# Gates and half of q as seven products of halves per pair of column tiles, with V and the gates kept in DRAM

## The chip, the core and the metric

The kernel runs on one core of one Trainium2 chip. The core has five engines with queues of their own: TensorE (PE) multiplies, VectorE (DVE), ScalarE (ACT) and GpSimd (POOL) work on tiles, and SyncE (SP) issues most of the transfers between DRAM and the core's memory (SBUF). Matmul results go to PSUM, eight banks of 128x512 float32 numbers. Each engine takes its instructions in the order in which the program has them and waits on semaphores for the others. The metric is the device time of one execution in microseconds (us), the median of several runs.

## What is computed

One layer on 1024 tokens of 1024 features, with 16 learned meta tokens ahead of them, in float32. The normed rows u go through one wide projection, and three branches are gated and merged; a mixture of experts follows.

```python
p = u @ w_in
a, bv, bg, q, k, v, fg, gates = jnp.split(p, ...)
ya = pool_mixer(a, ...) @ w_out_a
yb = conv_module(bv, bg, ...) @ w_out_b        # 31 taps, layer norm, swish
logf = jax.nn.log_sigmoid((fg + b_forget).astype(jnp.float32))
yc = forgetting_attention(heads(q), heads(k), heads(v), logf) @ w_out_c
g = jax.nn.sigmoid(gates.reshape(B_, L, N_BRANCH, D))
merged = g[:, :, 0] * ya + g[:, :, 1] * yb + g[:, :, 2] * yc
h = h + merged @ w_o
h = h + hier_moe(rms_norm(h))                   # 16 experts, two of a group's four for a token
```

The gates are 3 x 1024 columns of the projection, 24 column tiles of 128; q, k and v have four each, a, bv and bg two each.

## The kernel before

Float32 accuracy comes from two parts of each operand. A helper, split, makes the high part on ACT (a cast, L167) and the low part on DVE (a subtraction, L168); mm3 (L173) then multiplies high by high, low by high and high by low. A column tile of the projection for 512 tokens is 8 blocks of features times 3 kinds, 24 matmuls of 128x128 by 128x512. The normed u lies transposed in four tiles (two high, two low), each with four blocks of 1040 tokens.

The projection is a list of jobs, run by run_jobs in order, with the weights of a job loaded and split some jobs ahead. The order is bg, bv and a, then four times K and Q of a pair of heads, the 16 gate tiles of branches A and B, V with the forget gate, and the 8 gate tiles of branch C, the last of them among the first attention scores. Each K and Q goes to DRAM (dq, dk) as high and low part. Vector work of the pooling branch and of the convolution is queued in a list, pending: the pooling, 60 taps (L446), the layer norm (L455 to L498, with matmuls against ones at L460 for sums over channels). Its pieces are taken off the list ("pumped") a few at a time behind each job; before the gates the list is emptied.

A gate tile's sigmoid (L548) meets its branch at once: mm_bk gets a product with w_out_a or w_out_b (6 matmuls a half tile), DVE multiplies (L554, L557), POOL adds (L558). The merged rows (mg4) and the gates of C stay in SBUF, as V does. Attention works in units of a head's half, in blocks of 128 tokens: scores (L754, L755), exp, transposes (L803), weighing of V (L812, L814); heads are loaded by SP (L716 to L723) one ahead. Behind it the third branch (L860 to L872) and the output projection (L1095) follow, then routing and experts. SBUF is handed out in 12 equal slots; a freed slot goes to the next taker, whose first write waits for the last use. The order of instructions on an engine is settled when the program is built, so it can differ a little from the order in the source.

Of the kernel before, what the change touches and what calls it, by code (L numbers as in the profile page):

```python
# [7 lines left out]
F32 = mybir.dt.float32  # L8
# [33 lines left out]
def view(a, off, shape, dt=None):  # L42
    """A piece of a [P, n] tile, from column `off`, in `shape`"""
    n = 1
    for s in shape:
        n *= s
    a = a[:, off:off + n]
    if dt is not None:
        a = a.bitcast(dt)
    if len(shape) == 2:  # L50
        a = a.rearrange("p (a b) -> p a b", b=shape[1])
    elif len(shape) == 3:
        a = a.rearrange("p (a b c) -> p a b c", b=shape[1], c=shape[2])
# [15 lines left out]
class Slot:  # L69
    """A tile whose columns are handed out from the left"""  # L70
# [35 lines left out]
class Banks:  # L106
    """A ring over PSUM banks, `span` neighbours at a time."""
# [14 lines left out]
def body(tc, A, out):  # L122
# [3 lines left out]
    with es:  # L126
# [48 lines left out]
        def rms_stats(src, rows_, junk, st):  # L175
            """st[:, 2] <- 1/sqrt(mean(src^2) + eps)"""
# [46 lines left out]
        class UTile:  # L223
            """a tile of tokens on its way into u"""
# [66 lines left out]
        # background vector work, put between the matmul groups  # L291
# [76 lines left out]
        def run_jobs(js):  # L368
            """each job's weights are got ready `look` jobs ahead of it"""
# [18 lines left out]
        def start_b(_):  # L388
# [8 lines left out]
            queue_conv()  # L397

# [4 lines left out]
        def queue_pool():  # L403
# [31 lines left out]
            pending.append(lambda: s_at.free())  # L435

        def queue_conv():
# [13 lines left out]
            def both(x, ct):  # L451
                """the sum of the two halves of the channels, in two parts; they lie where the result will"""
# [23 lines left out]
            def ln_var():  # L476
# [8 lines left out]
                # 1 / sqrt, with a Newton step after the table's root  # L485
# [18 lines left out]
            pending.extend([ln_sum, ln_mean, ln_var, lambda: ln_out(0), lambda: ln_out(1), ln_free])  # L504

        for hp in range(4):
            def kq(w, hp=hp, which=0):
# [20 lines left out]
        def MG(dt):
            return st["mg4"][dt // 4][:, dt % 4, :]

        job(lambda: None, start_g)

        def gate(w, dt, c):
            g = proj(w, *REAL_CHUNKS[c])
            return g

        def out_unit(wname, nk, dt):
            wv = A[wname][0].rearrange("(k p) c -> p k c", p=P)
            return load_unit(wv[:, :, dt * P:(dt + 1) * P], nk, P, st["wr"])

        def branch(b, dt, w, wy, y, nk):
            yh, yl = y[:, 0], y[:, 1]
            hy, ly = wy
            for c in range(2):
                cs = slice(c * 512, c * 512 + 512)
                g = proj(w, *REAL_CHUNKS[c])
                sg = st["sig"].next([512])
                ac.activation(sg, g, AF.Sigmoid)  # L548
                o = mm_bk.next()
                mm3(o, [hy[:, k, :] for k in range(nk)], [ly[:, k, :] for k in range(nk)],  # L550
                    [yh[:, k, cs] for k in range(nk)], [yl[:, k, cs] for k in range(nk)])
                m = MG(dt)[:, cs]
                if b == 0:
                    ve.tensor_mul(m, sg, o)  # L554
                else:
                    t = st["prd"].next([512])
                    ve.tensor_mul(t, sg, o)  # L557
                    gp.tensor_add(m, m, t)  # L558

        for b, wn, key in ((0, "w_out_a", "yaT"), (1, "w_out_b", "ybT")):  # L560
            for dt in range(KT):
                def comp(w, b=b, dt=dt, key=key, wn=wn):
                    branch(b, dt, w, out_unit(wn, 2, dt), st[key], 2)
                job(lambda b=b, dt=dt: win_unit(COL_G + b * D + dt * P), comp)

# [1 line left out]
        def start_v(_):  # L567
            st["s_ya"].free(), st["s_yb"].free(), st["s_mi"].free()
            # V by heads, high and low part side by side
            st["s_vo"] = [sl.take(F32R), sl.take(F32R)]  # L570
            st["vo"] = [x.new([2, 2 * S]) for x in st["s_vo"]]
# [6 lines left out]
        def v_put(o, m, j, h0, nh, d0, d1):  # L578
            """heads h0.. of V, columns d0 to d1 of each, from o: both parts into their place"""
            if j == 8:  # L580
                hi, lo = (st["v8"][:m, h0:h0 + nh, t, d0:d1] for t in range(2))
            else:
                v = st["vo"][h0 // 4].rearrange("p q (j h t d) -> p q j h t d", j=8, h=2, t=2)
                v = v[:m, :, j] if nh == 4 else v[:m, h0 // 2 % 2, j]
                if nh == 1:
                    v = v[:, h0 % 2:h0 % 2 + 1]
                hi, lo = (v[:, :, :, t, :] if nh == 4 else v[:, :, t, d0:d1] for t in range(2))
            if nh == 4 and j < 8:
                o = o.rearrange("p (q h d) -> p q h d", h=2, d=HD)
            else:  # L590
                o = o.rearrange("p (h d) -> p h d", d=d1 - d0)
            split(o, hi, lo)
# [1056 lines left out]
```

## Time and profile before

| | |
|---|---|
| median of 3 runs | 1184.94 us (1184.16 to 1185.47) |
| span of the profiled execution | 1188.1 us |
| PE busy in it | 1084.6 us, 91%, 5585 matmuls |
| DVE, ACT, POOL busy | 713.7, 462.0, 316.4 us |
| granted TensorE clock, 240 to 400 us | 1.00 |

The profile is of one execution, the span is its time from first to last instruction, and it lies a little above the median of the timed runs. A page of it gives busy times and the costliest groups; the trace can also be asked for a timeline of one engine, for windows of time with the busy time of each engine, and for groups by line and shape. [...] In a timeline row an entry in brackets is idle time before the row and what ended it.

### The profile page before, as it was taken

Reading aid. Unit: us, or ns where it says so; the run is one execution under the profiler, and the core shown is the slowest. Engines: PE = TensorE matmul, PEld = TensorE weight load, DVE = VectorE, ACT = ScalarE, POOL = GpSimd, SP = SyncE. Lnnn points to the kernel's source line nnn. Section 1 sums busy time; section 2 is a strip of 40 time slices with the busy share of each in tenths; the row PEclk is TensorE's granted clock in tenths of the full one; section 3 lists DMA queues with packets and bytes.
Section 4 is the critical chain, followed back from the end, with each engine's and each line's share of the span. In section 5 each row is a group of like instructions: output and inputs, shape, how many; then the busy total and the mean of one; then the engine's idle time right before and its main releaser. Section 6 shows DMA issues by size and latency. Waiting matters only on the chain. (4 is left out here: it accounts for less than half of the span.)

```text
span 1188.1 us, 15991 instructions
## 1 busy us (share of the span) xinstructions
PE 1084.6 (91%) x5585; PEld 903.8 (76%) x5585; DVE 713.7 (60%) x1274; ACT 462.0 (39%) x845; POOL 316.4 (27%) x399
## 2 busy tenths in 40 slices
PE   5999999999999999999999999899956988988872
PEld 5999897888888898887888878677745766766651
DVE  5799965712112223112888867677786955758864
ACT  5412224311122123223888852322324634536541
POOL 4001221000111200001333226200143844635654
PEclk9999999999999999999999999999967989989986
DMA  7412443211111110105855242633576896786963
GB/s 224 119 54 89 130 147 98 67 45 45 45 46 41 46 44 4 37 1 126 207 136 134 65 133 98 213 143 142 178 261 216 269 311 169 186 275 190 298 219 141
DMA packets 92547, 160.13 MB, mean 135 GB/s; under 512 B 10625, under 2 KB 59858, under 8 KB 92420
## 3 DMA queue, kind: packets, MB, share of 16 engines
q1 hardware_dynamic: 82356, 130.08, 35.5%
q0 software_dynamic: 9632, 26.94, 8.5%
q10 hardware_dynamic: 432, 1.57, 0.4%
q8 instruction: 61, 1.00, 0.3%
q14 instruction: 66, 0.54, 0.1%
HBM read 127.97 MB, written 37.33 MB: 139 GB/s over the span
## 5 line engine op out<-in xcount | busy, mean ns | idle before, releaser
L173 PE MATMUL ps<-slot,slot 128*128 128x512 f32 (+3 forms) x2016 | 423.9, 369 | 0.9 <-ACT slot L247 0.9
L173 PEld LDWEIGHTS ps<-slot,slot 128*128 128x128 f32 x2016 | 358.0, 189 | 59.2 <-ACT slot L247 1.4
L168 DVE TENSOR_TENSOR slot<-slot,slot 128x1024 fp32r<-128x1024 f32 (+2 forms) x146 | 189.2, 1322 | 141.8 <-PE ps L173 124.8
L167 ACT CAST slot<-slot 128x1024 fp32r<-128x1024 f32 (+2 forms) x163 | 151.9, 974 | 197.5 <-PE ps L173 115.2
L173 PE MATMUL ps<-slot,sm 128*128 128x512 f32 x468 | 133.8, 429 | 29.6 <-DVE sm L1344 27.9
L1328 PE MATMUL ps<-slot,slot 128*128 128x512 f32 x552 | 140.3, 411 | 14.2 <-PEq L1610 7.0
L1328 PEld LDWEIGHTS ps<-slot,slot 128*128 128x128 f32 x552 | 107.4, 198 | 45.2 <-issue 13.2
L173 PEld LDWEIGHTS ps<-slot,sm 128*128 128x128 f32 x468 | 93.0, 205 | 54.9 <-DVE sm L1344 32.4
L168 DVE TENSOR_TENSOR slot<-ps,slot 128x512 fp32r<-128x512 f32 (+3 forms) x174 | 85.9, 515 | 36.3 <-ACT slot L167 35.3
L1095 PE MATMUL ps<-slot,slot 128*128 128x512 f32 x384 | 98.5, 401 | 1.5 <-ACT slot L167 1.5
L167 ACT CAST slot<-ps 128x512 fp32r<-128x512 f32 (+3 forms) x174 | 75.2, 449 | 50.0 <-PE ps L607 23.7
L168 POOL TENSOR_TENSOR slot<-slot,slot 128x1024 fp32r<-128x1024 f32 x32 | 83.6, 2632 | 4.3 <-ACT slot L167 4.0
L1095 PEld LDWEIGHTS ps<-slot,slot 128*128 128x128 f32 x384 | 68.7, 188 | 14.5 <-ACT slot L167 1.9
L446 DVE SCALAR_TENSOR_TENSOR slot<-slot,c,slot 128x1024 f32<-128x1024 f32 x60 | 74.9, 1278 | 0.6
L558 POOL TENSOR_TENSOR slot<-slot,slot 128x512 f32<-128x512 f32 x16 | 21.4, 1335 | 197.1 <-DVE slot L557 197.1
L760 DVE CUSTOM_DVE_ANT_0 slot<-ps,slot 128x656 f32<-128x656 f32 (+7 forms) x64 | 49.4, 772 | 33.2 <-PE ps L755 19.7
L803 PE MATMUL ps<-const,slot 128*128 128x128 f32 x352 | 59.1, 276 | 0.9 <-ACT slot L692 0.4
L548 ACT ACTIVATE slot<-ps 128x512 f32<-128x512 f32 x32 | 19.2, 600 | 94.6 <-PE ps L173 92.2
L762 ACT ACTIVATE slot<-slot,sm 128x656 f32<-128x656 f32 (+7 forms) x64 | 50.8, 794 | 10.5 <-DVE sm L760 10.4
L607 PE MATMUL ps<-slot,slot 128*128 128x260 f32 (+1 forms) x432 | 51.7, 282 | 0.0
L607 PEld LDWEIGHTS ps<-slot,slot 128*128 128x128 f32 (+1 forms) x432 | 50.5, 178 | 1.2
L803 PEld LDWEIGHTS ps<-const,slot 128*128 128x128 f32 x352 | 41.9, 140 | 8.4 <-issue 1.4
(275 smaller groups left out, 1333.6 us busy)
## 6 DMA issues: line engine op xcount, KB each, us to landing
slot<-in_exp_w_dram SPq DMA_DIRECT2D x96, 512.0 KB
slot<-in_w_in_dram SPq DMA_DIRECT2D x38, 512.0 KB
slot<-dk SPq DMA_DIRECT2D x32, 260.0 KB
slot<-in_x_dram SPq DMA_DIRECT2D x16, 512.0 KB
slot<-dF SPq DMA_DIRECT2D x8, 520.0 KB
dq<-slot POOLq DMA_DIRECT2D x16, 256.0 KB, 2.3
slot<-dq SPq DMA_DIRECT2D x16, 256.0 KB
slot<-in_w_o_dram SPq DMA_DIRECT2D x8, 512.0 KB
```

The source lines that it names most:

```text
L167: ac.copy(hi, raw)
L168: (lo_eng or ve).tensor_sub(lo, raw, f32(hi))
L173: pe.matmul(o, a, b, start=i == 0, stop=i == len(ops) - 1)
L446: ve.scalar_tensor_tensor(acc[:, ct, :], src, wk, acc[:, ct, :], ALU.mult, ALU.add)
L548: ac.activation(sg, g, AF.Sigmoid)
L558: gp.tensor_add(m, m, t)
L607: pe.matmul(o, u, w, start=i == 0, stop=i == len(ops) - 1)
L760: ve.tensor_tensor_reduce(out=s2, in0=o, in1=n2, scale=-1.0, scalar=3.0e38, op0=ALU.add, op1=ALU.min, accum_out=mn)
L762: return lambda: ac.activation(s[:, 0:w], s[:, 0:w], AF.Exp, bias=mn, scale=-1.0, accum_out=sm[:, 8 + i:9 + i])
L803: pe.transpose(tp[:, t * P:(t + 1) * P], p_of(g, i0 + t)[:, b * P:(b + 1) * P], ident)
L1095: pe.matmul(o[:, c, :], a, b, start=n == 0, stop=n == 23)
L1328: pe.matmul(o, x[:, k, :], wk, start=q == 0 and i == 0, stop=q == 1 and i == len(ops) - 1)
```

## The change

Two column tiles next to each other (256 columns of weights) times two halves of the tokens and two halves of the features form a product of 2x2 blocks. It was made with eight products of blocks and is now made with seven, with sums of blocks on both sides (the scheme of Strassen and Winograd). Four sums of weights (s1 to s4) are made per pair by POOL; the sums of quarters of u are the same for all pairs and are made once on DVE (queue_sums and the head of seven): tq[3], tq[2] and tq[4], each in high and low part, and one that overwrites a quarter of u. Scratch for them, x and y, lies in one slot, s_wx, which later serves as the ring for the weights' sums. PSUM collects products that share terms; a partial result is copied out (kept) and added (joined) where it enters two results. Thirteen pairs are made so: column tiles 2 and 3 of q, and the 24 gate tiles.

The order is now bg, bv and a, four K tiles, V with the forget gate, two q tiles, the thirteen pairs. V (dv) and the gates' sigmoids (dg) are written to DRAM and read back; so are the results of the pooling and the convolution (dy, by spill). Attention follows the last pair. The products of A and B with w_out_a and w_out_b stand behind attention now, ahead of those of C.

```diff
+        dv = dr.tile([S, NH * 2 * HD], F32, name="dv")
+        dg = dr.tile([3, KT, P, S], F32, name="dg")
+        dy = [dr.tile([P, 4 * S], F32, name=f"dy{b}") for b in range(2)]
...
+        def spill(b, key):
+            x = st["s_" + key]
+            sy.dma_start(dy[b], f32(x.ap[:, 0:4 * S]))
+            x.free()
...
             pending.extend([ln_sum, ln_mean, ln_var, lambda: ln_out(0), lambda: ln_out(1), ln_free,
+                            lambda: spill(1, "yb")])
...
+        def queue_sums():
+            def begin():
+                st["s_t"] = [sl.take(F32R) for _ in range(3)]
+                st["s_wx"] = sl.take()
...
+                st["x"], st["y"] = (view(st["s_wx"].ap, o, [4, 512]) for o in (2048, 0))
...
+            def parts(n, of):
+                return [lambda: ac.copy(tq[n][0], st[of]),
+                        lambda: ve.tensor_sub(tq[n][1], st[of], f32(tq[n][0]))]
+            pending.extend(diff("x", 1, 1, 0, 1, "y") + parts(3, "x") + diff("x", 0, 1, 0, 0, "y") +
+                           less("y", 1, 1, "x") + parts(2, "y") + less("y", 1, 0, "y") + parts(4, "y"))
...
+        for hp in range(4):
+            qk_job(COL_K, hp, 0, 13)
...
+        job(lambda: [win_unit(COL_V + half * 260, 260, k0, k0 + 4) for half in range(2) for k0 in (0, 4)], v_all, 1)
...
+        job(lambda: None, forget)
+        qk_job(COL_Q, 0, 1, 4, 1)
+        qk_job(COL_Q, 1, 1, 4)
+        PAIRS = [("q", 2)] + [(b, dt) for b in range(3) for dt in range(0, KT, 2)]
+        def seven():
+            pump(1000)
+            ac.copy(uq(0, 0, 1), st["x"])
+            ve.tensor_sub(uq(1, 0, 1), st["x"], f32(uq(0, 0, 1)))
+            right = {1: (uq(0, 0, 0), uq(1, 0, 0)), 2: (uq(0, 1, 0), uq(1, 1, 0)), 3: (uq(0, 1, 1), uq(1, 1, 1)),
+                     4: tq[4], 5: (uq(0, 0, 1), uq(1, 0, 1)), 6: tq[2], 7: tq[3]}
+            st_raw = Ring([s_raw.ap[:, n * 2048:n * 2048 + 2048] for n in range(2)])
+            st_sum = Ring([st["s_wx"].ap[:, n * 2048:n * 2048 + 2048] for n in range(2)])
...
+                gp.tensor_sub(s3, a[0, 0], a[1, 0])
+                gp.tensor_add(s1, a[1, 0], a[1, 1])
+                gp.tensor_sub(s2, s1, a[0, 0])
+                gp.tensor_sub(s4, a[0, 1], s2)
...
+            def bank(n, m):
+                return ps[:, (5 if (len(PAIRS) - 1 - n) % 2 == 0 else 0) + {2: 1, 7: 2, 4: 2}.get(m, 0), :]
+            def product(n, m):
...
+                ops = [(x, y, k) for x, y in ((hi, rh), (lo, rh), (hi, rl)) for k in range(4)]
...
+            def kept(n, key, m):
+                tmp[n, key] = t_r.next([512])
+                ac.copy(f32(tmp[n, key]), bank(n, m))
...
+                ac.activation(t, x, AF.Sigmoid)
+                sy.dma_start(dg[b, i + d, :, cs], t)
...
+            for n in range(len(PAIRS)):
+                order += [(n, 7), (n, 6), (n, 2), (n, 5)]
+                if n + 1 < len(PAIRS):
+                    order.append((n + 1, 1))
+                order += [(n, 3), (n, 4)]
...
+                if n == len(PAIRS) - 1:
+                    if m == 6:
...
+                        attention_start()
+                    if m == 5:
+                        s_u[0].free(), s_u[2].free()
+                        load_v()
+                        first_scores()
...
+        def load_branches():
+            for q in range(2):
+                sy.dma_start(st["mg4"][q], dg[0, q * 4:q * 4 + 4].rearrange("k p s -> p k s"))
+            for b in range(2):
+                sy.dma_start(f32(s_br[b].ap[:, 0:4 * S]), dy[b])
...
+        def unit_out(n):
...
+                if b == 0:
+                    ve.tensor_mul(m, m, o)
+                else:
+                    t = gates[n][:, cs]
+                    ve.tensor_mul(t, t, o)
+                    gp.tensor_add(m, m, t)
...
+        def load_gate(n):
+            if KT <= n < len(units):
+                gates[n] = gate_r.next([S])
+                sy.dma_start(gates[n], dg[units[n][0], units[n][1]])
...
+        for n in range(4, 2 * KT):
+            unit_out(n)
+            if n >= KT:
+                load_gate(n + 4)
```

How the order of instructions changes is shown at three places; a row gives the line in the kernel, the operation, output and inputs, the size, and the semaphores it waits for. First DVE around the end of the layer norm, in the kernel before (slot_1417 is the result of the convolution in two parts, slot_746 its work, slot_1463 the merged rows):

```order
L495 TENSOR_TENSOR slot_746<-slot_746,slot_93 128x1024 [waits DVE_49]
L495 TENSOR_TENSOR slot_746<-slot_746,slot_93 128x1024
L496 TENSOR_SCALAR slot_746<-slot_746,c_2_71 128x1024 [waits DVE_49] x2
L168 TENSOR_TENSOR slot_88<-slot_86,slot_87 128x1024 [waits DMAHW1_49,PE_49,Activation_49]
L498 TENSOR_TENSOR slot_746<-slot_746 128x1024 [waits Activation_49] x2
L168 TENSOR_TENSOR sm_24_1466<-slot_1465,sm_24_1466 128x256 [waits DMAHW7_49,PE_49]
L168 TENSOR_TENSOR slot_1417<-slot_746,slot_1417 128x1024 [waits Activation_49] x2
L554 TENSOR_TENSOR slot_1463<-slot_1465,ps 128x512 [waits DVE_49]
L554 TENSOR_TENSOR slot_1463<-slot_1465,ps 128x512 x2
L554 TENSOR_TENSOR slot_1463<-slot_1465,ps 128x512 [waits Activation_49]
L554 TENSOR_TENSOR slot_1463<-slot_1465,ps 128x512 [waits PE_49,Activation_49]
```

Behind the last split into slot_1417 come the products with the first gates. In the changed kernel (slot_1720 is the convolution's result, slot_1907 the scratch for the sums, slot_93 to slot_96 are u, slot_1905 is tq[3]) the same place reads:

```order
L509 TENSOR_TENSOR slot_750<-slot_750 128x1024 [waits Activation_49] x2
L1140 CAST c_54_5602<-c_54_5602 128x8 [waits Pool_49]
L172 TENSOR_TENSOR slot_1720<-slot_750,slot_1720 128x1024 [waits Activation_49]
L689 TENSOR_TENSOR slot_749<-ps,slot_749 128x512 [waits PE_49,Activation_49]
L172 TENSOR_TENSOR slot_1720<-slot_750,slot_1720 128x1024 [waits Activation_49]
L700 SCALAR_TENSOR_TENSOR slot_749<-slot_749 128x512 [waits Activation_49]
L535 TENSOR_TENSOR slot_1907<-slot_94,slot_93 128x2048 [waits DMAHW5_49,DVE_49]
L536 TENSOR_TENSOR slot_1907<-slot_96,slot_95 128x2048
L537 TENSOR_TENSOR slot_1907<-slot_1907 128x2048 [waits DVE_49]
L536 TENSOR_TENSOR slot_1907<-slot_95 128x2048 [waits DVE_49]
L546 TENSOR_TENSOR slot_1905<-slot_1907,slot_1905 128x2048 [waits Activation_49]
L535 TENSOR_TENSOR slot_1907<-slot_93 128x2048 [waits DVE_49]
```

The sums of u follow the last split. The wait on DMAHW5 in the first of them is for the store of slot_1720 to DRAM on SP (L445), whose place in SBUF slot_1907 takes.

Second, PE at the layer norm's matmuls (L460; slot_89 to slot_92 are u, slot_87 and slot_88 parts of weights, slot_747 and sm_24 those of the pooling branch and its output weights), before:

```order
L173 MATMUL ps<-slot_89,slot_88 128x512 x4
L173 MATMUL ps<-slot_90,slot_88 128x512 x4
L173 MATMUL ps<-slot_89,slot_87 128x512 [waits DVE_49]
L173 MATMUL ps<-slot_89,slot_87 128x512 x3
L173 MATMUL ps<-slot_90,slot_87 128x512 x4
L460 MATMUL ps<-slot_1417,ones_80 128x512 [waits Activation_49]
L460 MATMUL ps<-slot_1417,ones_80 128x512
L173 MATMUL ps<-slot_747,sm_24_1466 128x512 [waits Activation_49]
L173 MATMUL ps<-slot_747,sm_24_1466 128x512 x2
L460 MATMUL ps<-slot_1417,ones_80 128x512 [waits DVE_49]
L460 MATMUL ps<-slot_1417,ones_80 128x512
```

They stand among the first gate tiles. In the changed kernel those matmuls (L471) stand right behind V, and further on, behind the q tiles, the first of the seven products (L680, slot_91 and slot_92 the parts of the weights) read:

```order
L680 MATMUL ps<-slot_95,slot_91 128x512 x4
L680 MATMUL ps<-slot_94,slot_92 128x512 [waits DVE_49]
L680 MATMUL ps<-slot_94,slot_92 128x512 x3
L680 MATMUL ps<-slot_96,slot_91 128x512 x4
L680 MATMUL ps<-slot_93,slot_91 128x512
L680 MATMUL ps<-slot_93,slot_92 128x512 x4
L680 MATMUL ps<-slot_95,slot_91 128x512 x4
L680 MATMUL ps<-slot_1905,slot_91 128x512 [waits Activation_49]
L680 MATMUL ps<-slot_1905,slot_91 128x512 x3
L680 MATMUL ps<-slot_1905,slot_92 128x512 [waits DVE_49]
L680 MATMUL ps<-slot_1905,slot_92 128x512 x3
L680 MATMUL ps<-slot_1905,slot_91 128x512 x4
```

The first product with a sum of u (slot_1905) is the fourth, and waits for ACT.

Third, SP around the loads of head 1, before (L191 loads weights, L716 to L718 a head's q and k, L723 its forget terms):

```order
L191 DMA slot_86<-in_w_in_dram 128x8x128 [waits DMAHW2_49,DVE_49]
L191 DMA slot_86<-in_w_in_dram 128x8x128 [waits DMAHW3_49,DVE_49]
L716 DMA slot_3495<-dq 64x1024 [waits DMAHW4_49,DMAHW3_49,DMAHW5_49,DMAHW2_49,DVE_49]
L717 DMA slot_3495<-dk 64x1040
L718 DMA slot_3495<-dk 64x1040 [waits DMAHW6_49]
L716 DMA slot_3495<-dq 64x1024 [waits DMAHW7_49]
L717 DMA slot_3495<-dk 64x1040 [waits DMAHW0_49]
L718 DMA slot_3495<-dk 64x1040 [waits DMAHW1_49]
L723 DMA slot_3562<-dF 128x656 [waits DMASW0_49,PE_49]
L723 DMA slot_3562<-dF 128x1040
L723 DMA slot_3562<-dF 128x656 [waits DMAHW4_49,DMAHW2_49,DVE_49]
L716 DMA slot_3633<-dq 64x1024 [waits DMAHW5_49,PE_49]
```

and in the changed kernel (L707 writes gates, L750 reads V, L773 to L775 a head's q and k):

```order
L707 DMA dg<-slot_749 128x512 [waits DMAHW7_49,Activation_49]
L707 DMA dg<-slot_749 128x512 [waits DMAHW0_49,Activation_49]
L750 DMA slot_3437<-dv 128x8x256 [waits DMASW7_49,DMASW6_49,DMAHW1_49,DMASW3_49,PE_49]
L750 DMA slot_3437<-dv 128x8x256 [waits DMAHW2_49]
L750 DMA slot_3438<-dv 128x8x256 [waits DMAHW3_49,PE_49]
L750 DMA slot_3438<-dv 128x8x256 [waits DMAHW4_49]
L707 DMA dg<-slot_749 128x512 [waits DMAHW5_49,Activation_49]
L707 DMA dg<-slot_749 128x512 [waits DMAHW6_49,Activation_49]
L773 DMA slot_3499<-dq 64x1024 [waits DMAHW7_49,DVE_49,PE_49]
L774 DMA slot_3499<-dk 64x1040 [waits DMAHW0_49]
L775 DMA slot_3499<-dk 64x1040 [waits DMAHW1_49]
L773 DMA slot_3499<-dq 64x1024 [waits DMAHW2_49]
```

The four reads of V have come in ahead of head 1, whose loads are those into slot_3499, and the last gates are written between.

## Rows read from the trace of the kernel before

**Rows 1.** The page's head, and part 1: busy us, share and instructions by engine.
```profile
span 1188.1 us, 15991 instructions
...
PE 1084.6 (91%) x5585; PEld 903.8 (76%) x5585; DVE 713.7 (60%) x1274; ACT 462.0 (39%) x845; POOL 316.4 (27%) x399
```

**Rows 2.** Windows by stage: us, busy of PE, PEld, DVE, ACT, POOL; clock, DMA, GB/s.
```profile
189.00:414.00 225.00, 224.83 (x973) 181.95 (x972) 73.40 (x87) 54.02 (x77) 21.40 (x18) 1.00 0.18 50
414.00:470.00 56.00, 55.86 (x449) 53.48 (x448) 15.79 (x60) 16.20 (x52) 2.12 (x3) 1.00 0.11 29
470.00:558.00 88.00, 86.83 (x377) 69.65 (x378) 11.65 (x29) 19.16 (x29) 5.14 (x34) 1.00 0.17 42
```

**Rows 3.** Timeline of PE: start, us, line, tiles, matmuls.
```profile
120.90 68.06 PE L173 MATMUL ps<-slot,slot 128*128 128x400 f32 x360
188.80 1.10 PE L460 MATMUL ps<-slot,ones 128*128 128x512 f32 x4
...
232.81 5.73 PE L173 MATMUL ps<-slot,slot 128*128 128x512 f32 x24
238.38 1.55 PE L173 MATMUL ps<-slot,sm 128*128 128x512 f32 x6
```

**Rows 4.** Windows of DVE's early and later work, columns as in rows 2.
```profile
60.00:100.00 40.00, 40.00 (x254) 39.99 (x253) 39.66 (x36) 7.05 (x12) 0.00 (x0) 1.00 0.14 40
...
240.00:400.00 160.00, 160.00 (x692) 129.75 (x691) 34.40 (x47) 30.91 (x46) 17.49 (x13) 1.00 0.16 44
```

**Rows 5.** Timeline of DVE in the layer norm: start, us, line, operation.
```profile
190.80 2.47 DVE L473 SCALAR_TENSOR_TENSOR slot<-ps,slot 128x512 f32<-128x512 f32 x4
...
211.94 0.69 DVE L490 TENSOR_SCALAR slot<-slot 128x1024 f32<-128x1024 f32 x1
...
213.93 2.36 DVE L495 TENSOR_TENSOR slot<-slot,slot 128x1024 f32<-128x1024 f32 x2
...
222.72 2.35 DVE L168 TENSOR_TENSOR slot<-slot,slot 128x1024 fp32r<-128x1024 f32 x2
```

**Rows 6.** The page's costliest groups: busy, mean ns of one, idle before.
```profile
L558 POOL TENSOR_TENSOR slot<-slot,slot 128x512 f32<-128x512 f32 x16 | 21.4, 1335 | 197.1 <-DVE slot L557 197.1
...
L607 PE MATMUL ps<-slot,slot 128*128 128x260 f32 (+1 forms) x432 | 51.7, 282 | 0.0
```

**Rows 7.** The page's DMA issues: count, KB each, us to landing.
```profile
dq<-slot POOLq DMA_DIRECT2D x16, 256.0 KB, 2.3
```

**Rows 8.** Windows of transfers, attention and clock, columns as in rows 2.
```profile
600.00:700.00 100.00, 96.68 (x643) 84.30 (x642) 83.64 (x194) 85.30 (x199) 29.29 (x84) 1.00 0.50 125
...
870.00:880.00 10.00, 1.93 (x9) 1.40 (x8) 8.94 (x38) 2.84 (x5) 3.26 (x3) 0.50 0.84 297
880.00:890.00 10.00, 6.92 (x23) 5.62 (x24) 9.19 (x13) 3.93 (x5) 8.12 (x6) 0.52 0.87 302
...
565.00:575.00 10.00, 8.53 (x57) 7.07 (x56) 7.77 (x18) 7.68 (x20) 3.22 (x10) 1.00 1.04 241
```

**Rows 9.** Groups by line and shape, ACT and DVE: busy, mean ns of one.
```profile
L167 ACT CAST slot<-slot 128x1024 fp32r<-128x1024 f32 x131 | 131.3, 1047 | 144.4 <-PE ps L173 97.2 <-PEq L1610 12.7 <-issue 10.0
...
L167 ACT CAST slot<-slot 128x512 fp32r<-128x512 f32 x28 | 16.9, 618 | 35.1 <-DVE slot L870 15.0 <-PE ps L1095 7.6 <-DVE slot L431 5.3
...
L168 DVE TENSOR_TENSOR slot<-slot,slot 128x512 fp32r<-128x512 f32 x28 | 20.6, 735 | 2.8 <-ACT slot L167 2.8
```

**Rows 10.** Timeline of PE after the output projection, columns as in rows 3.
```profile
882.91 1.25 PE L1316 MATMUL ps<-ones,slot 128*128 128x128 f32 x8 [5.39 <-DMA slot<-dT,lists]
...
885.78 7.03 PE L1328 MATMUL ps<-slot,slot 128*128 128x512 f32 x22
```

**Rows 11.** Timeline of SP: the first load of head 1.
```profile
558.28 0.45 SPq L716 DMA_DIRECT2D slot<-dq  x1
```

**Rows 12.** Timeline of PE: the first scores of head 1.
```profile
568.99 0.46 PE L754 MATMUL ps<-slot 128*128 128x328 f32 x2
```

More of the change, by code (lines that the diff above doesn't have):

```diff
@@ L528, in MG @@
[L528 to L564, printed above, removed]
+                pump(n)
+            job(lambda: win_unit(col + hp * P), comp, look)
+        for hp in range(4):
+            qk_job(COL_K, hp, 0, 13)
         def start_v(_):
[L568 to L571 removed]
+            st["vt"] = Ring([st["s_qk"].ap[:, n * 1024:n * 1024 + 1024] for n in range(4)])
@@ L576, in start_v @@
             gp.memset(st["lf"], 0.0)
[L578 to L592, printed above, removed]
@@ L697, in body, with load_v @@
+        def load_v():
+            st["s_vo"] = [sl.take(F32R) for _ in range(2)]
+            st["vo"] = [x.new([2, 2 * S]) for x in st["s_vo"]]
+            for hp in range(4):
+                sy.dma_start(f32(st["vo"][hp // 2][:, hp % 2, :]).rearrange("p (j c) -> p j c", c=256),
+                             dv.rearrange("(j p) c -> p j c", p=P)[:, :, hp * 256:hp * 256 + 256])
         heads, late = {}, []
         def attention_start():
-            st["s_s"] = sl.take()
+            st["s_k1"], st["s_s"] = sl.take(F32R), sl.take()
@@ L765, in body @@
         run_jobs(jobs)
-        for x in s_u[:2] + [st["s_hl"]]:
-            x.free()
+        seven()
         s_vo, vo, v8 = st["s_vo"], st["vo"], st["v8"]
@@ L907, in body @@
         mm_bk = Banks(ps, 0, 8)
-        groups = [(dt, c) for dt in range(KT) for c in range(2)]
-        first = {gr: yc_part(gr, 0) for gr in groups[:3]}
-        for f in late:
-            f()
-        for x in (s_k1, s_k3, s_o, s_p):
+        gates = {}
+        for n in range(4):
+            unit_out(n)
+            if late:
+                late.pop(0)()
+        assert not late
+        for x in (s_k1, s_k3, s_o, s_p):
+            x.free()
+        s_gr = sl.take()
+        gate_r = s_gr.ring(S, 4)
+        def load_gate(n):
+            if KT <= n < len(units):
+                gates[n] = gate_r.next([S])
+                sy.dma_start(gates[n], dg[units[n][0], units[n][1]])
+        for n in range(4):
+            load_gate(KT + n)
+        for n in range(4, 2 * KT):
+            unit_out(n)
+            if n >= KT:
+                load_gate(n + 4)
+        for x in s_br:
             x.free()
@@ L921, in body @@
         w_o = A["w_o"][0].rearrange("(k p) c -> p k c", p=P)
-        for dt, c in groups:
-            if c == 0:
-                if 0 < dt < KT - 1:
-                    wc[dt + 1] = out_unit("w_out_c", 4, dt + 1)
-                raw = raw_r.next([D])
-                sy.dma_start(raw, w_o[:, dt, :])
-                split(raw, WO(0, dt), WO(1, dt))
-            yc_out((dt, c), first.pop((dt, c), None))
-        for x in s_vo + st["s_gc"] + [s_y1, s_y2]:
+        for n in range(2 * KT, 3 * KT):
+            dt = units[n][1]
+            raw = raw_r.next([D])
+            sy.dma_start(raw, w_o[:, dt, :])
+            split(raw, WO(0, dt), WO(1, dt))
+            unit_out(n)
+            load_gate(n + 4)
+        for x in s_vo + [s_gr, s_y1, s_y2]:
             x.free()
```

232 lines of the change are left out of this document (134 added, 98 removed).

## The prediction

> **What bounds the kernel now.** I read the head of the page first: a span of 1188.1 us in which TensorE (PE) is busy 91% and VectorE (DVE) 60% [rows 1]. An average hides stages, so the second view is the table of windows by stage: between 189 and 558 us PE works 224.83 of 225 us, 55.86 of 56 and 86.83 of 88, always at a granted clock of 1.00, while DVE has 73 of 225 us to do in the longest of them [rows 2]. The reader should see there that a matmul taken away in this stretch is time won, one for one, and that any wait in front of a matmul is time lost, since there is no idle time to absorb it. Third is PE's timeline: 24 matmuls of 128x512 start at 232.81 and the next group at 238.38, so one costs 5.57 / 24 = 0.232 us [rows 3]. Last I looked at who could make PE wait. DVE is full early, with the convolution's taps (39.66 of 40 us from 60 to 100), and has 34.40 of 160 to do later [rows 4]. Behind the taps comes the convolution's layer norm: one chain, DVE to ScalarE (ACT) to PE and back, from the matmuls of its mean at 188.80 to the end of the last split at 222.72 + 2.35 = 225.1, that is 36.3 us [rows 3, 5]. It is latency more than load, and it costs nothing now only because PE multiplies gate tiles beside it; what needs its result comes many products later.
>
> **The change, part by part.** *Fewer matmuls.* A pair of column tiles took 2 tiles x 2 halves of the tokens x 24 = 96 matmuls. It now takes 7 products of 4 x 3 = 84. There are 13 pairs (one of q, twelve of gates): 13 x 12 = 156 matmuls, 156 x 0.232 = 36.2 us won.
>
> *The order ahead of the products.* V now follows the four K tiles, and the q tiles come later. In the trace three K and three q tiles (360 matmuls) run from 120.90 to 188.80, 67.9 / 6 = 11.3 us each, and V's matmuls are 51.7 us [rows 3, 6]. What stood ahead of 188.80, less four q tiles, plus V, ends at 188.8 - 45.2 + 51.7 = 195.3. By the order of instructions the matmuls of the layer norm's mean come right behind V (0.9 us), then two q tiles (22.6) among the forget gate's small matmuls (1) and short waits for it (2, an estimate), then three products on plain quarters of u (36 x 0.232 = 8.4), which wait for copies that stand on DVE behind parts of the layer norm (2.5, an estimate from two of its operations of 1.2 us [rows 5]). PE has nothing left that is ready at 195.3 + 0.9 + 22.6 + 1 + 2 + 8.4 + 2.5 = 232.7, say 233; 4.5 us of that are waits.
>
> *What it then waits for.* Every other product needs a sum of quarters of u. Before, some 190 us of gate products followed the layer norm on PE; now the sums follow it at once in DVE's queue. The norm starts when V ends and takes the 36.3 us of before, plus about 1 for the forget gate's operations in the same queue: 233. Its last split completes the tile that SP stores to DRAM (2 MB), and the scratch for the sums takes that tile's place, so DVE's next instruction waits for the store to land. No row shows a store of 2 MB. One of 256 KB takes 2.3 us [rows 7], and below that it can't be; 2 MB at the 302 GB/s of a busy window take 6.9 us, at the 241 GB/s of another 8.7 [rows 8]. I take 8.7 + 0.5 = 9.2, by the slower row, since issue and landing come on top: the sums begin at 242.2.
>
> [...]
>
> A sum is a tensor_tensor over 2048 columns, which no row shows either. Two over 1024 take 2.36 us together, 1.18 each [rows 5]. If length cost nothing, 2048 would take 1.18; at twice the time, 2.36. I take 2.2, near the upper end, since one start is saved.
>
> [...]
>
> The first matmul on a sum (tile slot_1905) also needs a sum of weights, which POOL writes over x in the scratch tile, and so after the ninth sum on DVE: 9 x 2.2 = 19.8, a POOL subtraction 1.3 and an ACT cast 0.6 make 21.8 [rows 6, 9]. It runs at 264.0, and PE stands idle 264.0 - 233 = 31. One product follows (2.8). The next belongs to the first pair, whose sums of weights are written over y, and the chain needs y to its end: five more sums (11.0), three short splits between them (2.2), two ACT copies of 2048 columns (twice 1.05 each at most, of which I count 4 in all as exposed), then POOL and cast again (1.9): 19.1. PE idles 19.1 - 2.8 = 16.3. With the 4.5 above, 31 + 16.3 + 4.5 = 51.8 us lost.
>
> [...]
>
> *The steady pairs.* A pair is 84 x 0.232 = 19.5 us of PE. Beside it lie 7 casts, 3 kept copies and 4 sigmoids on ACT (14 x 0.6 = 8.4), 7 splits and 3 joins on DVE (10 x 0.74 = 7.4), 4 sums on POOL (4 x 1.34 = 5.4) [rows 6, 9] and 1 MB in and 1 MB out (108 GB/s). PE waits for a kept copy only with another product (2.8) between. I cost the pairs at nothing; if that cover is gone, it is a rival below.
>
> *Attention.* V (4 MB) comes back from DRAM, and on SP its four loads stand ahead of head 1's. Before, head 1's first load was issued at 558.28 and its scores ran at 568.99 [rows 11, 12]. 4 MB at 241 GB/s take 17 us; about 11 lie under the last four products. The other 6, and 6 MB of gates and branches read in the middle ahead of one head's loads, meet a PE that has 3.3 us of idle in 100 there [rows 8]: I take 4 (bounds 0 and 15).
>
> *Behind attention.* The 192 matmuls of branches A and B only move (192 x 0.232 = 44.5 us). POOL's two adds of 1.34 a unit [rows 6] just fit beside a unit's 2.8 us of PE, and eight PSUM banks take up what sticks out: nothing, at most 3.
>
> The total on the profiled execution: 1188.1 - 36.2 + 51.8 + 4 + 4 = 1211.7. Its span lies 3.2 us above the median of the runs, 1184.94, so the forecast for the median is 1208.5, or 1209.
>
> **The rivals.** *A short chain (faster).* The place is DVE between V's end and the last sum. Were the norm a quarter shorter, with no other tile's splits in between (27 us), the store done in the 2.3 us of the small one, and the sums as fast per column as the one-source operation at 211.94 (0.69 for 1024 [rows 5], so 1.4), the sums would begin at 224.6, the first dependent product could run at 239.1, and the gaps would be 6 and 12.3: -36.2 + 18.3 + 4.5 + 2 = -11.4, a time of 1174. The chain decides from the point where both gaps stay under 30 us together (36.2 - 4.5 - 2). For it: part of the 36.3 us is waiting and others' work. Against it: the sums read two tensors, as the 1.18 us operations do. *Stalled pairs.* If a kept copy, or a cast behind a late sum of weights, made PE wait one product's length in each pair, 12 x 2.8 = 34 us more: 1243. For it: several of the seven products go through one PSUM bank. Against it: no engine beside PE is half full in a pair. *Reloads that collide.* 10 MB at 241 GB/s are 41 us; with a third of it uncovered, 14 in place of 4: 1219. *Half the wait.* Gaps of 28 to 32 leave the time where it is: 1185.
>
> **How the numbers follow.** The forecast gets 0.58, the reloads 0.09, stalled pairs 0.12, half the wait 0.06 and the short chain 0.15. The forecast's own range: at the low end the store 6.9 (2.3 less), sums at 2.1 (1.4 less), the small waits gone (4.5), 1 for the clock and 0 for attention, 1193; at the high end sums at 2.36 (2.2 more), 6 us more of the norm, 8 and 15, 1232. Reaching down to half the wait and up toward the stalled pairs gives 1184 to 1238, which leaves out most of the short chain and half of the stalled pairs, 0.2. A measurement of this kernel tells about 0.2%, 2.4 us, from no change. Faster holds the short chain and a little of half the wait, 0.17; same 0.05; slower 0.78.
>
> **What would show it.** In the profile after, PE has two gaps right behind the first three products, and DVE's first sum waits for the store; the clock falls to 0.50 there. There are 156 matmuls fewer, and the later pairs run at 19.5 us. Attention begins about 25 us before the old time, since 44.5 us moved behind it and about 20 came in. The forecast is wrong if the gaps stay under 30 us, or if later pairs take over 20 us each.

## The result and the profile after

The changed kernel takes 1219.85 us (median of 4 runs, 1217.87 to 1221.37) against 1184.61 before on the same chip: a ratio of 1.030, 95% interval 1.0284 to 1.0316, 35 us slower. The forecast was 1209, with a range of 1184 to 1238.

The head of the page and PE's costliest group, which answer to [rows 1] and [rows 6]:

```profile
span 1216.2 us, 16197 instructions
...
PE 1059.8 (87%) x5429; PEld 883.2 (73%) x5429; DVE 804.1 (66%) x1383; ACT 517.2 (43%) x943; POOL 398.2 (33%) x459
...
L680 PE MATMUL ps<-slot,slot 128*128 128x512 f32 x1092 | 264.0, 404 | 54.3 <-ACT slot L171 46.1
```

PE has 156 matmuls fewer and 24.8 us less busy time, yet its share has fallen from 91 to 87%. The seven products (L680) were kept waiting 54.3 us, 46.1 of it by casts on ACT. The spans differ by 28.1 us and the medians by 35.2: the execution of before that was profiled ran above its median, that of the changed kernel 2 us below its own, and in the former the later stages, alike in both kernels, were 8 us longer (442.0 us from the first matmul of the output projection to the end, 434.0 after).

PE's timeline at the head of the products (start, us, line, tiles, matmuls, idle time before and what ended it) shows where they wait:

```profile
195.99 1.09 PE L471 MATMUL ps<-slot,ones 128*128 128x512 f32 x4
...
222.09 2.02 PE L680 MATMUL ps<-slot,slot 128*128 128x512 f32 x8
225.94 8.32 PE L680 MATMUL ps<-slot,slot 128*128 128x512 f32 x28 [1.83 <-DVE slot L291]
266.09 5.33 PE L680 MATMUL ps<-slot,slot 128*128 128x512 f32 x12 [31.82 <-ACT slot L171]
285.71 9.66 PE L680 MATMUL ps<-slot,slot 128*128 128x512 f32 x29 [14.30 <-ACT slot L171]
299.99 18.21 PE L680 MATMUL ps<-slot,slot 128*128 128x512 f32 x67 [4.62 <-ACT slot L685]
319.25 214.26 PE L680 MATMUL ps<-slot,slot 128*128 128x512 f32 x924 [1.04 <-ACT slot L685]
```

The norm's mean (L471) stands behind V, at 195.99. After 36 matmuls of products PE idles 31.82 us, does one product, idles 14.30 and, some two products later, 4.62 more. Then it runs on: the last row's 924 matmuls took 214.26 us, 0.232 each. The windows (us, busy of PE, PEld, DVE, ACT, POOL; clock, DMA, GB/s) add the clock (the granted share of TensorE's full clock), where [rows 2] had 1.00 throughout:

```profile
233.00:266.00 33.00, 1.26 (x6) 0.69 (x4) 24.26 (x12) 5.60 (x5) 4.93 (x4) 0.56 0.19 79
266.00:271.00 5.00, 4.91 (x12) 3.80 (x12) 2.98 (x3) 1.64 (x4) 3.83 (x3) 0.50 0.00 0
271.00:273.00 2.00, 0.41 (x2) 0.00 (x0) 0.89 (x2) 1.44 (x1) 0.00 (x0) 0.98 0.02 4
276.00:285.00 9.00, 0.00 (x0) 0.00 (x0) 5.67 (x3) 1.90 (x1) 1.25 (x2) 0.50 0.00 0
285.00:291.00 6.00, 5.29 (x12) 4.13 (x13) 4.88 (x4) 2.48 (x4) 4.45 (x4) 0.50 0.05 4
292.00:298.00 6.00, 3.38 (x15) 2.41 (x13) 0.58 (x1) 0.00 (x0) 2.94 (x3) 1.00 0.37 130
299.00:305.00 6.00, 5.01 (x12) 3.94 (x13) 1.81 (x2) 1.46 (x3) 1.16 (x1) 0.50 0.00 0
306.00:320.00 14.00, 12.96 (x56) 10.16 (x55) 7.30 (x11) 6.73 (x13) 5.80 (x8) 1.00 0.61 206
345.00:540.00 195.00, 194.32 (x841) 157.27 (x840) 71.30 (x93) 78.83 (x134) 47.62 (x45) 1.00 0.36 117
```

The clock falls in each of the three gaps and comes back behind each: it is 0.50 at 266 to 271, 285 to 291 and 299 to 305, for some twelve matmuls each time, and 0.98 to 1.00 at 271 to 273, 292 to 298 and from 306 on. The three groups of matmuls behind the gaps took 5.33, 9.66 and 18.21 us for 12, 29 and 67 matmuls, 2.5, 2.9 and 2.7 us more than at 0.232 each, 8.1 together. From 345 to 540 PE works 194.32 of 195 us, with DVE, ACT and POOL under half busy: the pairs themselves wait for nothing.

What PE waits for is on DVE (same columns as PE's timeline):

```profile
232.89 1.22 DVE L172 TENSOR_TENSOR slot<-slot,slot 128x1024 fp32r<-128x1024 f32 x1
...
241.53 2.29 DVE L535 TENSOR_TENSOR slot<-slot,slot 128x2048 f32<-128x2048 f32 x1 [6.83 <-DMA dy<-slot]
243.75 2.29 DVE L536 TENSOR_TENSOR slot<-slot,slot 128x2048 f32<-128x2048 f32 x1
...
259.78 2.28 DVE L640 TENSOR_TENSOR slot<-slot,slot 128x2048 fp32r<-128x2048 f32 x1
261.98 2.28 DVE L542 TENSOR_TENSOR slot<-slot,slot 128x2048 f32<-128x2048 f32 x1
...
281.38 2.29 DVE L546 TENSOR_TENSOR slot<-slot,slot 128x2048 fp32r<-128x2048 f32 x1 [1.96 <-ACT slot L545]
```

The norm's last split ends at 234.1. The first sum starts 7.4 us later, released by the store to DRAM, and from then on the sums follow each other at 2.29 us each. The ninth (L640) ends at 262.06; POOL's first sum of weights and a cast stand between it and the product at 266.09:

```profile
262.15 3.23 POOL L659 TENSOR_TENSOR slot<-slot 128x512 f32<-128x512 f32 x1 [26.61 <-DVE slot L640]
265.35 1.26 POOL L660 TENSOR_TENSOR slot<-slot 128x512 f32<-128x512 f32 x1
...
283.75 1.26 POOL L659 TENSOR_TENSOR slot<-slot 128x512 f32<-128x512 f32 x1 [13.76 <-DVE slot L546]
...
294.98 1.27 POOL L659 TENSOR_TENSOR slot<-slot 128x512 f32<-128x512 f32 x1 [5.37 <-DMA slot<-in_w_in_dram]
```

The last of these rows belongs to the third gap: POOL had waited 5.37 us for the third pair's weights from DRAM, whose load SP had issued only at 289.63; ACT's casts for that pair waited for POOL, and the copy that PE needed stood behind them on ACT.

Attention's first transposes run at 544.3 (559.5 before) and its last weighing at 689.0 (697.7), 144.7 us against 138.2; from there to the output projection it is 93.2 against 48.4, 44.8 more.

### The profile page after: what moved, and what is told of

The parts are those of the page before. It is cut to its first block, busy times and chain, and to the rows that moved or that the text cites. A ratio compares the mean times of both kernels' runs of the same rounds, so it can differ in the third digit from the quotient of the medians.

```text
span 1216.2 us, 16197 instructions
## 1 busy us (share of the span) xinstructions
PE 1059.8 (87%) x5429; PEld 883.2 (73%) x5429; DVE 804.1 (66%) x1383; ACT 517.2 (43%) x943; POOL 398.2 (33%) x459
## 5 line engine op out<-in xcount | busy, mean ns | idle before, releaser
L680 PE MATMUL ps<-slot,slot 128*128 128x512 f32 x1092 | 264.0, 404 | 54.3 <-ACT slot L171 46.1
L172 DVE TENSOR_TENSOR slot<-slot,slot 128x512 fp32r<-128x512 f32 (+3 forms) x227 | 233.6, 1048 | 117.0 <-ACT slot L171 112.0
L680 PEld LDWEIGHTS ps<-slot,slot 128*128 128x128 f32 x1092 | 211.0, 194 | 106.6 <-ACT slot L171 47.1
L171 ACT CAST slot<-slot 128x512 fp32r<-128x512 f32 (+3 forms) x244 | 188.0, 797 | 218.4 <-PE ps L177 77.0
L177 PE MATMUL ps<-slot,slot 128*128 128x512 f32 (+3 forms) x1200 | 228.0, 350 | 2.1 <-ACT slot L251 1.2
L177 PEld LDWEIGHTS ps<-slot,slot 128*128 128x128 f32 x1200 | 204.1, 189 | 22.8 <-ACT slot L251 1.7
L1422 PE MATMUL ps<-slot,slot 128*128 128x512 f32 x552 | 141.0, 411 | 19.0 <-PEq L1704 10.5
L1422 PEld LDWEIGHTS ps<-slot,slot 128*128 128x128 f32 x552 | 107.7, 198 | 50.1 <-issue 16.8
L172 DVE TENSOR_TENSOR slot<-ps,slot 128x512 fp32r<-128x512 f32 (+6 forms) x166 | 84.8, 533 | 28.5 <-ACT slot L171 27.6
L1189 PE MATMUL ps<-slot,slot 128*128 128x512 f32 x384 | 99.5, 405 | 3.8 <-ACT slot L171 3.8
L177 PE MATMUL ps<-slot,sm 128*128 128x512 f32 x276 | 81.2, 443 | 24.2 <-DVE sm L1438 22.8
L171 ACT CAST slot<-ps 128x512 fp32r<-128x512 f32 (+6 forms) x166 | 74.3, 464 | 54.1 <-PE ps L587 27.5
L177 PEld LDWEIGHTS ps<-slot,sm 128*128 128x128 f32 x276 | 55.1, 210 | 40.4 <-DVE sm L1438 27.0
L1189 PEld LDWEIGHTS ps<-slot,slot 128*128 128x128 f32 x384 | 69.9, 191 | 16.7 <-ACT slot L171 3.9
L689 DVE TENSOR_TENSOR slot<-ps,slot 128x512 f32<-128x512 f32 x39 | 27.0, 691 | 51.6 <-PE ps L680 29.6
```

Of the source, the lines that this page charges most:

```text
L171: ac.copy(hi, raw)
L172: (lo_eng or ve).tensor_sub(lo, raw, f32(hi))
L177: pe.matmul(o, a, b, start=i == 0, stop=i == len(ops) - 1)
L680: pe.matmul(o, x[:, k, :], y[:, k, :], start=i == 0 and m in (1, 2, 7), stop=i == 11 and m in (2, 3, 4), skip_group_check=True)
L689: ve.tensor_add(t, bank(n, m), t)
L1189: pe.matmul(o[:, c, :], a, b, start=n == 0, stop=n == 23)
```

## The experiments

The theory: the loss is PE's idle time at the head of the products, which is the length of one chain (norm, store, sums of u, sums of weights) less the work that lies beside it, and the low clock (0.50) behind the gaps. The main rival: the moves cost it (V, gates and branches through DRAM, two branches behind attention). All times are medians beside runs of the kernel before on the same chip (1182.3 to 1185.0).

**e1, the store out of the chain.** The scratch slot takes the place that is free first:

```diff
-                st["s_t"] = [sl.take(F32R) for _ in range(3)]
                 st["s_wx"] = sl.take()
+                st["s_t"] = [sl.take(F32R) for _ in range(3)]
```

> The scratch slot of the sums is taken ahead of the three slots for their results, so it gets the place of the pooling's result, stored long before, and the first sum no longer waits for the 2 MB store of the convolution's result. Theory (PE's two gaps at the head of the products are the length of the chain norm, store, sums): the 6.8 us that DVE waited for the store go, the first gap shrinks from 31.8 to about 25, the time falls by 7 from 1219.9 to about 1213. Rival (the gaps are set by something else, such as the weights' sums on POOL): no change, 1220.

Measured: 1199.6 (1199.1 to 1204.4), ratio to before 1.0145 (1.0119 to 1.0170). That is 20 us less, not 7. PE's timeline:

```profile
227.21 4.97 PE L680 MATMUL ps<-slot,slot 128*128 128x512 f32 x20 [1.84 <-DVE slot L291]
239.60 3.78 PE L680 MATMUL ps<-slot,slot 128*128 128x512 f32 x8 [7.42 <-DVE slot L172]
247.98 5.49 PE L680 MATMUL ps<-slot,slot 128*128 128x512 f32 x12 [4.60 <-ACT slot L171]
268.08 9.75 PE L680 MATMUL ps<-slot,slot 128*128 128x512 f32 x29 [14.62 <-ACT slot L171]
```

The gap of 31.8 has become 7.42 and 4.60; the second, 14.62, has stayed. DVE's timeline shows why it was more than the wait for the store:

```profile
165.17 2.28 DVE L535 TENSOR_TENSOR slot<-slot,slot 128x2048 f32<-128x2048 f32 x1
...
175.04 2.28 DVE L536 TENSOR_TENSOR slot<-slot 128x2048 f32<-128x2048 f32 x1
...
227.07 2.33 DVE L546 TENSOR_TENSOR slot<-slot,slot 128x2048 fp32r<-128x2048 f32 x1
...
229.92 2.35 DVE L509 TENSOR_TENSOR slot<-slot 128x1024 f32<-128x1024 f32 x2
232.19 2.28 DVE L535 TENSOR_TENSOR slot<-slot 128x2048 f32<-128x2048 f32 x1
```

The first four sums, of 2.28 us each, now run at 165 to 177 beside V's matmuls, ahead of the whole norm. The fifth (L546, at 227.07) stands ahead of the norm's last multiplications (L509) and the sixth (L535, at 232.19) ahead of its splits. The scratch is free from the pooling's store on, so these sums no longer wait for a store. So one wrong slot had cost the wait and also the order: nothing that uses the slot could go ahead of its store.

**e2, the norm earlier.**

```diff
-                pump(3)
+                pump(6)
```

> Six pieces of queued vector work are put behind each tile of V instead of three, so the norm's mean stands in PE's order after the fifth tile of V and not behind the ninth. Theory: the whole chain starts about 23 us earlier (4 tiles of 5.7 us), PE reaches the products at the same time as before, the gaps fall from 46 to about 23 together, and the time is about 1197, or 1194 if the low clock lasts less. Rival (vector work put into V makes V's own copies wait, and PE with them): V gets 5 to 15 us longer and half or more of the gain is gone, 1205 to 1212.

Measured: 1198.4 (1193.7 to 1201.2), ratio 1.0138 (1.0097 to 1.0178), 21 us less, as the theory had it. The mean's matmuls run at 173, V's own matmuls stay dense, and the gaps:

```profile
173.07 1.08 PE L471 MATMUL ps<-slot,ones 128*128 128x512 f32 x4
...
246.06 5.12 PE L680 MATMUL ps<-slot,slot 128*128 128x512 f32 x12 [8.77 <-ACT slot L171]
266.14 9.27 PE L680 MATMUL ps<-slot,slot 128*128 128x512 f32 x29 [14.96 <-ACT slot L171]
```

The first gap has shrunk from 31.82 to 8.77, the second is 14.96: it lies within the sums and doesn't care when they start.

**e3, the moves alone.** Every column tile is made plainly, with no sums (the function for q tiles and gates, in short):

```diff
-            queue_sums()
...
-        seven()
+        def plain(b, dt):
+            def comp(w):
+                for c in range(2):
...
+                    o = proj(w, *REAL_CHUNKS[c])
+                    t = f32(qk_r.next([512]))
+                    ac.activation(t, o, AF.Sigmoid)
+                    sy.dma_start(dg[b, dt, :, cs], t)
+            job(lambda: win_unit(COL_G + b * D + dt * P), comp)
```

> All column tiles are made plainly (24 matmuls a half tile), without sums of u; V and gates still go through DRAM, and branches A and B still stand behind attention. So it has 156 matmuls more (36.2 us) and no chain for PE to wait for. Theory (the loss is the gaps, 52 us of idle and 8 us of low clock): 1219.9 - 60 + 36 = 1196, with attention's 6.5 us more than before left in it; at least 1190. Rival (the moves through DRAM and behind attention cost most of it): over 1205.

Measured: 1184.2 (1181.2 to 1191.2), ratio 1.0015 (0.9988 to 1.0042): the same as before, 12 us under what the theory gave and far from the rival. PE runs through the place of the gaps:

```profile
211.02 49.19 PE L177 MATMUL ps<-slot,slot 128*128 128x512 f32 x211
```

The moves cost nothing that shows (by the interval 1 us less to 5 us more): the whole loss of 35 us, and the 36 us of the matmuls saved on top, went with the seven products. Attention takes 136.5 us here, against 144.7; the four slots that the sums would take are free, and the order of SP has V's reads at 226 to 253 and the first read of gates just ahead of attention. So the theory was wrong to leave "attention's 6.5 us more than before" in it: they come with the products, too, and are 8 of the 12 us; the other 4 are not accounted for.

**e4, e1 and e2 together.**

> The edits of e1 and e2 together: the scratch in a slot that is free early, and six pieces of vector work behind each tile of V. Theory: the two savings add, 7 + 23 and some of the low clock: gaps of about 16 us and a time of 1187 to 1190. Rival (each only lays bare the other's wait, or the weights' sums on POOL): no better than the better of the two, about 1196.

Measured: 1175.8 (1174.2 to 1177.5), ratio 0.9940 (0.9920 to 0.9959), 44 us less than the changed kernel and 8.5 less than before: the two savings add (20 and 21 us), and the place of the wait moves. The theory's 1187 to 1190 was 11 us too high, since it put e1's saving at 7.

```profile
216.31 16.70 PE L177 MATMUL ps<-slot,slot 128*128 128x512 f32 x64 [10.53 <-DVE sm L593]
...
236.90 0.67 PE L615 MATMUL ps<-sm,c 128*128 128x72 f32 x2 [2.98 <-DVE sm L619]
...
250.21 0.30 PE L624 MATMUL ps<-const,sm 128*72 128x128 f32 x1 [2.75 <-DVE sm L622]
```

There is no gap in front of a product any more. PE waits 10.53 us within the first q tile, for V's last copies (L593), which now stand behind the sums on DVE, and twice for the forget gate.

**e5, another order.** With e1, and behind V's tiles and the q tiles:

```diff
-                pump(3)
+                pump(6 if j < 5 else 2)
...
-        qk_job(COL_Q, 0, 1, 4, 1)
-        qk_job(COL_Q, 1, 1, 4)
+        qk_job(COL_Q, 0, 1, 6, 1)
+        qk_job(COL_Q, 1, 1, 6)
```

> As e4, but the vector work behind V's tiles is six pieces for the first five tiles and two for the others, and six behind each of the two q tiles, so the norm starts as early as in e4 while most sums stand behind V's copies in DVE's queue. In e4 PE still waited 10.5 us at the first q tile for V's last copies, which stood behind nine sums on DVE, and some 6 us for the forget gate. Theory (what is left is order on DVE, not its amount): these go, a gap of up to 5 us may come back at the first product with a sum, and the time falls by 8 to 13 to 1163 to 1168. Rival (from the norm to the products DVE has more work than PE covers, whatever the order): the wait only moves to the products, 1173 to 1177.

Measured: 1179.0 (1177.6 to 1185.4), ratio 0.9963 (0.9941 to 0.9984). The theory fails here: no better than e4 (their ratios' intervals overlap), not 8 to 13 us faster. The rival's mechanism fits, though the time lies 2 us above its range.

```profile
210.24 9.24 PE L177 MATMUL ps<-slot,slot 128*128 128x512 f32 x32 [3.91 <-DVE sm L593]
...
241.62 2.50 PE L680 MATMUL ps<-slot,slot 128*128 128x512 f32 x5 [7.27 <-ACT slot L171]
247.09 25.29 PE L680 MATMUL ps<-slot,slot 128*128 128x512 f32 x99 [2.98 <-ACT slot L171]
275.84 44.53 PE L680 MATMUL ps<-slot,slot 128*128 128x512 f32 x185 [3.46 <-ACT slot L685]
```

The wait in the q tile is 3.91 in place of 10.53, but 7.27, 2.98 and 3.46 us are back at the products: 17.6 us in these waits, where e4 had 16.3. From V's end to the first product with a sum DVE has more to do than PE covers; the order only says where PE waits for it.

**e6, more cover.** As e5, with the last two q tiles made plainly ahead of the pairs:

```diff
+        qk_job(COL_Q, 2, 1, 3)
+        qk_job(COL_Q, 3, 1, 3)
...
-        PAIRS = [("q", 2)] + [(b, dt) for b in range(3) for dt in range(0, KT, 2)]
+        PAIRS = [(b, dt) for b in range(3) for dt in range(0, KT, 2)]
```

> As e5, and the last two q tiles are made plainly (48 matmuls more than seven products less 36, that is 12 matmuls or 2.8 us more in all), so 22 us of matmuls that need no sums stand ahead of the pairs. Theory (if a gap is left in e5, PE's cover was too short): the gap left goes, at a price of 2.8 us; with a gap of 5 in e5 the time is about 2 below e5, with none it is 3 above. Rival (amount of DVE's work bounds it): clearly below e5, by 6 or more.

Measured: 1164.7 (1163.4 to 1169.3), ratio 0.9838 (0.9805 to 0.9871), 14 us below e5 and 20 us faster than before, which of the other versions only e7 and e9, the same within their spread, reach. The waits that e5 still had at the products, 13.7 us together, are gone, and with them some 5 us of slower matmuls behind them (5, 99 and 185 in 2.50, 25.29 and 44.53 us, against 0.232 each in the steady pairs), for 2.8 us of added matmuls. The theory's 2 us was worked out for a gap of 5. The rival's number, 6 or more, came in; its reason is not shown, since DVE's work ahead of the pairs did not shrink here: the copies and splits of two q tiles joined it.

```profile
210.56 9.66 PE L177 MATMUL ps<-slot,slot 128*128 128x512 f32 x34 [3.92 <-DVE sm L593]
...
249.87 70.48 PE L682 MATMUL ps<-slot,slot 128*128 128x512 f32 x303
```

**e7, V's last copies first.** As e6, with `pump(6 if j < 5 else 1 if j < 8 else 0)`.

> As e6, but behind V's tiles six to eight one piece of vector work each and none behind the ninth, so that V's last copies stand ahead of the first sums on DVE. In e6 PE waited 3.9 us at the first q tile for those copies and ran the q tile behind it at the lower clock. Theory (this wait is order on DVE): it falls to under 1 us and the time to 1159 to 1163. Rival (the wait's length is made up again later): 1164 to 1167.

Measured: 1165.8 (1161.6 to 1169.6), ratio 0.9836 (0.9804 to 0.9868). The wait in the q tile is gone (0.23), but one of 3.57 us in front of the first product has come in its place. The rival is right: what is left is a few us of DVE's work without cover.

```profile
202.40 16.72 PE L177 MATMUL ps<-slot,slot 128*128 128x512 f32 x71 [0.23 <-DVE slot L172]
...
230.80 1.45 PE L682 MATMUL ps<-slot,slot 128*128 128x512 f32 x4 [3.57 <-DVE slot L291]
```

**e8, cover alone.** The changed kernel with the q edit of e6 and nothing else.

> The changed kernel with one edit: the last two q tiles are made plainly behind the first two, ahead of the products, and twelve pairs are left. The chain norm, store, sums stays as it was, PE gets 22 us more that needs no sum, at a price of 2.8 us of matmuls. Theory (PE's loss is the chain's length less the work that lies beside it): the first gap falls from 31.8 to 10 to 14, the second stays at 14, the time is 1200 to 1204. Rival (the added copies and splits on DVE lengthen the chain by as much): 1215 to 1222.

Measured: 1201.3 (1198.0 to 1202.5), ratio 1.0136 (1.0096 to 1.0175), 18.5 us less than the changed kernel, as the theory had it.

```profile
268.29 4.70 PE L682 MATMUL ps<-slot,slot 128*128 128x512 f32 x12 [14.44 <-ACT slot L171]
287.91 9.04 PE L682 MATMUL ps<-slot,slot 128*128 128x512 f32 x29 [14.92 <-ACT slot L171]
302.37 17.96 PE L682 MATMUL ps<-slot,slot 128*128 128x512 f32 x69 [5.42 <-ACT slot L687]
```

The first gap falls from 31.82 to 14.44, by 17.4 for 22 us of other work. PE's matmuls ahead of it end 19.6 us later than in the changed kernel (253.9 for 234.3), and the product that it waits for comes 2.2 us later (268.29 for 266.09), as shorter operations now stand among the sums on DVE. The second and third gap (14.92, 5.42) stay.

**e9, V's reads behind head 1.** As e6, with three of V's four reads issued behind `heads[1] = load_head(1)`.

> As e6, with one edit at the start of attention: of V's four reads from DRAM only the first (two heads) stands ahead of head 1's loads on SP, the other three behind them. In e6 attention takes 146 us from its first transposes to its last weighing, where it took 138 before and 136.5 in e3, whose reads of V stood earlier. Theory (the 4 MB of V in front of head 1 make PE wait and fall to the low clock there): attention 138 to 141, the time 5 to 8 below e6, 1157 to 1160. Rival (6 MB of gates and branches read in the middle, or attention's own order, cost it): no change, 1163 to 1167.

Measured: 1166.3 (1159.4 to 1168.8), ratio 0.9854 (0.9821 to 0.9887): no change that can be told. Attention's start in e6 and then in e9 (columns of the windows):

```profile
488.00:494.00 6.00, 4.49 (x18) 3.43 (x19) 3.03 (x10) 5.61 (x10) 1.79 (x6) 0.76 1.09 347
494.00:504.00 10.00, 8.60 (x32) 7.30 (x32) 4.67 (x12) 6.03 (x16) 1.25 (x6) 0.50 1.06 264
```

```profile
488.00:494.00 6.00, 3.83 (x20) 2.71 (x19) 3.22 (x10) 4.85 (x10) 1.87 (x6) 1.00 0.40 115
494.00:504.00 10.00, 7.43 (x39) 6.53 (x40) 5.51 (x15) 7.24 (x17) 1.82 (x7) 0.83 1.03 272
```

The low clock is milder there (0.83 in place of 0.50), and attention takes 144.0 us against 146, not 138 to 141. So V's place in the queue is a small part of it at most. What makes attention 7.5 us longer than in e3 even here stays open; e3 differs in the time of V's reads, in a part of the gates' read and in the work right ahead of attention.

## Why the prediction was right

Direction, mechanism and range held; the forecast was 11 us short of the measured time, for a third gap that it had not and for a clock that cost twice what it had. By its steps:

- *Fewer matmuls.* Right: 5585 - 5429 = 156, and 0.232 us each in the steady pairs.
- *The order ahead of the products.* Forecast: V ends at 195.3, products start at about 222. Measured: 196.0 and 222.1.
- *The chain.* Norm to 233 (234.1), store 9.2 (7.4), sums 2.2 each (2.29), the first product with a sum at 264.0 (266.1). That the first gap came out at 31.8 for a forecast of 31 is luck, because errors met: the norm ended 1.1 later, the nine sums took 20.5 for 19.8, POOL's first subtraction took 3.23 us where [rows 6] have 1.34, the store was shorter by 1.8, and the work beside the chain ended at 234.3 for 233. The store's 9.2 came from the rate of a busy window; the trace has 7.4 from issue to release, 283 GB/s.
- *The second gap.* 16.3 forecast, 14.3 measured. From one product with a sum to the next it was 19.6 us for a forecast of 19.1, but the product between took 5.33 us at the low clock (0.50), not 2.8.
- *Missed: a third gap.* "I cost the pairs at nothing" holds from 320 us on, but the first pairs after the gaps waited 4.62 and 1.04 for kept copies, since casts stood ahead of them on ACT and waited for POOL, and POOL for weights. All idle time together: 55.1 us (with 0.85, 1.83 and 0.68 of small waits) against 51.8.
- *The clock, mis-sized.* 4 forecast, 8.1 measured. No run shows the 4 in the total, an estimate for two gaps. What the kernel before shows is 22 matmuls in 7.03 us behind a wait of 5.39 [rows 10], 1.9 more than at 0.232 each, or 3.9 for two such waits. In the changed kernel there were three restarts, since the third gap lost the clock again, and they cost 2.5, 2.9 and 2.7 us. The 2.5 of the first lay beside the chain and came off the second gap.
- *Attention's start.* Forecast 25 us ahead of the old time, measured 15 (544.3 for 559.5). Idle time (3.3 more than forecast) and clock (4.1 more) are most of the difference; 2.5 us are not accounted for.
- *Attention.* 4 forecast, 6.5 measured, within its bounds. The cause given, V's reads in front of head 1, is not shown by e9.
- *Behind attention.* 44.5 forecast for moved work, 44.8 measured.

So the sum is -36.2 + 55.1 + 8 + 6.5 = 33.4, against 35.2 between the medians. Of the rivals, the short chain was out by the first gap alone; half the wait is excluded by 46.1 us in the first two gaps, reloads that collide by 6.5 us in place of 14, and the "stalled pairs" by 194.32 of 195 us, though the third gap is their mechanism, a cast behind a late sum of weights, once.

The step that a reader should distrust is the length of the chain as one sum: e1 took one wait of 6.8 us out of it and won 20, because the order on DVE is settled when the program is built, and with the dependency gone four sums moved ahead of the norm.

## What to carry to other kernels

A saving on the engine that bounds a kernel needs its inputs ready: before work is put behind a chain, follow the chain from the last thing that covers it to the first instruction that needs it, and see what runs beside it. Work that needs nothing (here two plain q tiles) belongs in that place even when it costs more: e6 gave up 2.8 us of matmuls and won 14. And scratch that takes the place of something stored late puts the store, and all that the order could have moved, into the chain.

## What the runs showed of the hardware

- POOL's subtraction of two blocks of 128x512 in SBUF took 3.23 us (262.15 above) beside a DVE operation over two tiles in SBUF (L542, 261.98 above) that ended at 264.26, and 1.26 us without one (283.75). That is 1.97 us more beside it, and DVE's operation had 2.11 us to run when the subtraction began. The cause is not shown.
- After each of three gaps (31.8, 14.3 and 4.6 us) the clock was at 0.50 for some twelve matmuls and full again behind them; each restart cost 2.5 to 2.9 us.
- A 2 MB store from SBUF to DRAM, with 0.5 MB of other stores under way, took 7.4 us from issue (234.13) to the release of the engine that waits for it (241.53), 283 GB/s.
